# A 352-byte pad behind h's tile in place of 376 bytes, in a two-layer retention and convolution trunk on one core

## The chip, the core and the metric

The kernel runs on one core of a Trainium2 chip. The time is the device time of one execution in microseconds (us); the figure that counts is the median over runs. Before the change it is 2637.42 us (three runs, 2634.95 to 2639.48).

## What is computed

A trunk of two layers works on 256 tokens of width 2048 in f32. Layer 0 mixes tokens by multi-scale retention, layer 1 by a short gated convolution; each is followed by a SwiGLU feed-forward part (FFN), and every part is framed by an RMS norm with shift, scale and gate, which come from the conditioning vector `c`:

```python
for i in range(DEPTH):
    mod = (c_act @ w_mod[i] + b_mod[i])[:, None, :]
    sh1, sc1, g1, sh2, sc2, g2 = jnp.split(mod, 6, axis=-1)
    h = (rms_norm(x, norm1_g[i]) * (1.0 + sc1) + sh1)
    y = retention_mixer(...) if i == 0 else short_conv_mixer(...)
    x = x + g1 * y
    h = (rms_norm(x, norm2_g[i]) * (1.0 + sc2) + sh2)
    x = x + g2 * swiglu(h, ffn_w_in[i], ffn_w_out[i])
return rms_norm(x, final_g)
```

Nearly all of the work is products of an activation with a weight matrix: `h @ w_in` (retention: 2048 to 12288 columns, convolution: 2048 to 6144, FFN: 2048 to 11264) and then `mid @ w_out` back to 2048 columns.

## The kernel before

**Numbers in two parts.** Each f32 value is held as a high part that TensorE takes in its f32r type and the rest as a low part. A product is then three products: high by high, high by low, low by high. An activation tile is 128 rows by 2 x 256: the high part of the 256 tokens and behind it the low part, 2048 bytes in each partition. Weights arrive from memory as `raw` tiles of 128 x 2048, and `prepare` (lines 298 to 317) makes of each half of one a tile `hi` (ScalarE, line 313) and a tile `lo` (VectorE, line 316) of 128 x 1024, in four buffers each. A tile holds eight blocks of 128 x 128, each 512 bytes long in a partition, and `take` hands them out in the order of use.

**The products.** The loop of `product` (lines 348 to 366) makes one pair of matmuls for each weight block: line 358 loads the block of `hi` as the stationary operand and streams all 512 columns of the activation tile past it, line 361 loads the block of `lo` and streams the 256 columns of the high part. `packed` (lines 376 to 404) makes three matmuls of 256 columns instead (lines 398 to 400), for most of the retention's projections and for the last column of an output product; where the weights are 512 wide it hands over to `by_token` (lines 373 to 375), which loads `h` and streams the weights. `normed` (lines 506 to 553) has a form of its own for the first six columns after a norm, lines 529 to 531.

**The activations.** `h` is the normed input of each part. It is read by the input products of convolution and FFN, as the tile named `h` in lines 358 and 361. Their results become the `mid` tiles, 22 at a time in the FFN and 16 in the convolution, and the output products read those (`output`, lines 555 to 578). In the retention the tiles between input and output product are called `rm` (`rm_tile`, line 634); the output product over 32 of them comes in two parts, each after four heads.

**Where the tiles lie.** Pools are laid out in SBUF one behind the other, in the order in which they are opened, and each tile in them starts at a multiple of 32 bytes. The order is: constants, work tiles, the weights' pool (`raw`, `hi`, `lo`), the pool of `h` and, behind that, whatever is in use at the time: the retention's tiles (`rm`, `sin`, `cos`, the start's own `raw`, `q`, `k`, `v`, `sp`, `decay`, `sg`, `o`) or later those of FFN and convolution (`mid`, `silu`, `m`, `cu`, `y`, `out`). The pool of `h` holds three tiles: `aside` of 8 words (line 486), `h` itself, 17 x 514 words or 34952 bytes (line 487), and `beside`, which nobody reads or writes (line 488). The offsets in a partition are:

| tile | first byte | distance from the first `hi` | remainder by 512 |
|---|---|---|---|
| first `hi` (all `hi` and `lo` lie at multiples of 4096 from it) | 84832 | 0 | 0 |
| `h`, as FFN and convolution read it (`rows_at(0)`) | 117632 | 32800 | 32 |
| `h`, as the retention reads it (`rows_at(EARLIER)`, 480 bytes on) | 118112 | 33280 | 0 |
| first tile behind the pad; `rm` and `mid` tiles follow every 2048 bytes | 152992 | 68160 | 64 |

From here on "a distance of 64" means this remainder. The weights step by 512 bytes from block to block and the activations by 2048 from tile to tile, so the remainder stays what it is through a whole product.

**The order of work.** TensorE's instructions run in the order in which they are written out. The other engines' instructions are put in order by a planner; at the start, VectorE's and ScalarE's order is written out too. `prepare` runs two tiles ahead of TensorE (`AHEAD`). All loads go through SyncE's queue: `raw` of the weights, and `raw` of `w_mod` for the 192 columns of the modulation, each of which is one long VectorE instruction (line 247, and line 657 at the start, where the `raw` tile lies behind the pad).

Of the kernel before, what the change touches and what calls it, by code (L numbers as in the profile page):

```python
# [10 lines left out]
F32 = mybir.dt.float32  # L11
# [6 lines left out]
P = 128  # L18
# [170 lines left out]
def trunk(ctx: ExitStack, tc: tile.TileContext, x_in, c_in, pos_in, w_mod, cols_in, tab_in, w_all, out):  # L189
# [290 lines left out]
    hpool = ctx.enter_context(tc.tile_pool(name="hpool", bufs=1))  # L480
# [4 lines left out]

    hpool.tile([P, LEFT], F32, tag="aside", name="aside")
    h_all = hpool.tile([P, (KT + 1) * (ENDS + 2 * S)], F32R, tag="h", name="h")
    hpool.tile([P, 94], F32, tag="beside", name="beside")

    def rows_at(o):  # L490
        return [
# [575 lines left out]
```

## Time and profile before

| | |
|---|---|
| median of three runs | 2637.42 us |
| profiled execution | 2638.99 us, of which the span from first to last instruction is 2637.2 |
| granted TensorE clock | 0.997 over the span |
| TensorE busy | 2603.5 us |
| VectorE, ScalarE, GpSimd busy | 1989.3, 1248.5 and 149.3 us |
| moved by DMA | 687.58 MB |

A row of the page's groups gives line, engine and operation, the tiles (written from read), the shapes, the count, the busy time of the group in us, the mean duration of one instruction in ns, and the idle time of the engine ahead of the group with what ended it. The busy time counts a moment once, however many instructions of the group run in it. "PE" is TensorE's matmuls, "PEld" its weight loads, "DVE" VectorE, "ACT" ScalarE, "SP" SyncE. A view by windows gives, for stretches of the span, the busy time of each engine with its count of instructions, the granted clock, the busy share of the DMA engines and what they moved.

### The profile page before, as it was taken

How to read it: one execution, taken by the hardware profiler on the slowest of the kernel's cores; microseconds unless marked ns; L12 is line 12 of the kernel's file. 1: busy time of each engine (PE TensorE's matmuls, PEld its weight loads, DVE VectorE, ACT ScalarE, POOL GpSimd, SP SyncE). 2: the span in 40 equal slices, each digit the busy share in tenths (PEclk: the TensorE clock that was granted, in tenths of full speed). 3: DMA queues.
4: the chain of work that ended last, by engine and by line, in shares of the span. 5: the costliest groups of instructions: out<-in, count | busy, mean ns of one | idle time of the engine just before them, and what ended most of it. 6: DMA issues, size and time to landing. Idle time of an engine off the chain costs nothing.

```text
span 2637.2 us, 38238 instructions
## 1 busy us (share of the span) xinstructions
PE 2603.5 (99%) x15220; PEld 2304.2 (87%) x15220; DVE 1989.3 (75%) x2527; ACT 1248.5 (47%) x1788; POOL 149.3 (6%) x230
## 2 busy tenths in 40 slices
PE   7999999999999999999999999999999999999998
PEld 5988889888889888888888898888998888888887
DVE  7888878777698877777777889888886665555554
ACT  5544443444456444344444454444554443444443
POOL 0000001110000011110100001100000000000000
PEclk9999999999999999999999999999999999999999
DMA  9976768777686877777777768777777755555553
GB/s 399 384 278 244 254 249 299 276 267 276 238 307 249 315 284 280 261 285 287 287 273 276 265 226 323 284 285 257 254 273 269 255 217 184 191 192 191 189 181 126
DMA packets 96950, 687.58 MB, mean 261 GB/s; under 512 B 10753, under 2 KB 12545, under 8 KB 13825
## 3 DMA queue, kind: packets, MB, share of 16 engines
q1 hardware_dynamic: 96770, 685.13, 70.2%
q8 instruction: 119, 1.95, 0.3%
q14 instruction: 61, 0.50, 0.1%
HBM read 682.99 MB, written 2.10 MB: 260 GB/s over the span
## 4 chain that ended last, share of the span: by engine, by line
PE 75%; issue 20%; DVE 3%; DMA 2%; ACT 1%; POOL 0%; DVEq 0%; ACTq 0%; POOLq 0%
PE bank L358 34%; PE bank L361 18%; PE bank L373 4%; PE bank L374 4%; PE bank L375 4%; PE bank L400 2%; PE bank L399 2%; PE bank L398 2%; PE bank L529 1%; PE bank L531 1%; PE bank L530 1%; DVE raw L657 1%; DMA raw<-w_all 1%; DVE lo L316 1%; DMA raw<-w_mod 1%
## 5 line engine op out<-in xcount | busy, mean ns | idle before, releaser
L316 DVE TENSOR_TENSOR lo<-raw,hi 128x1024 fp32r<-128x1024 f32 x912 | 1112.0, 1222 | 544.9 <-ACT hi L313 543.7
L313 ACT CAST hi<-raw 128x1024 fp32r<-128x1024 f32 x912 | 953.6, 1050 | 1078.9 <-PE bank L358 648.3
L358 PE MATMUL bank<-h,hi 128*128 128x512 f32 x3296 | 1142.9, 390 | 0.0
L361 PE MATMUL bank<-h,lo 128*128 128x256 f32 x3296 | 929.5, 282 | 0.0
L358 PEld LDWEIGHTS bank<-h,hi 128*128 128x128 f32 x3296 | 618.8, 188 | 129.6
L361 PEld LDWEIGHTS bank<-h,lo 128*128 128x128 f32 x3296 | 622.9, 189 | 0.0
L358 PE MATMUL bank<-mid,hi 128*128 128x512 f32 x1604 | 566.2, 395 | 0.0
L361 PE MATMUL bank<-mid,lo 128*128 128x256 f32 x1604 | 452.1, 282 | 1.1 <-DVE lo L316 1.1
L247 DVE SCALAR_TENSOR_TENSOR raw<-raw,cb 128x2048 f32<-128x2048 f32 x160 | 365.3, 2283 | 14.9 <-DMA raw<-w_mod 14.6
L358 PEld LDWEIGHTS bank<-mid,hi 128*128 128x128 f32 x1604 | 301.4, 188 | 72.5
L361 PEld LDWEIGHTS bank<-mid,lo 128*128 128x128 f32 x1604 | 301.2, 188 | 1.5 <-DVE lo L316 1.5
L373 PE MATMUL bank<-hi,h 128*128 128x512 f32 x512 | 202.0, 395 | 0.0
L374 PE MATMUL bank<-lo,h 128*128 128x512 f32 x512 | 201.1, 393 | 0.0
L375 PE MATMUL bank<-hi,h 128*128 128x512 f32 x512 | 200.5, 392 | 0.0
L358 PE MATMUL bank<-rm,hi 128*128 128x512 f32 x496 | 175.3, 396 | 0.0
L400 PE MATMUL bank<-h,lo 128*128 128x256 f32 x512 | 146.3, 286 | 9.3 <-DVE lo L316 9.3
L398 PE MATMUL bank<-h,hi 128*128 128x256 f32 x512 | 145.9, 285 | 2.5 <-ACT h L685 2.5
L399 PE MATMUL bank<-h,hi 128*128 128x256 f32 x512 | 145.9, 285 | 0.5 <-DVE h L686 0.5
L361 PE MATMUL bank<-rm,lo 128*128 128x256 f32 x496 | 139.7, 282 | 0.0
L375 PEld LDWEIGHTS bank<-hi,h 128*128 128x128 f32 x512 | 96.8, 189 | 21.0
L358 PEld LDWEIGHTS bank<-rm,hi 128*128 128x128 f32 x496 | 93.2, 188 | 22.4
L373 PEld LDWEIGHTS bank<-hi,h 128*128 128x128 f32 x512 | 97.0, 189 | 18.0
(154 smaller groups left out, 2248.7 us busy)
## 6 DMA issues: line engine op xcount, KB each, us to landing
raw<-w_all SPq DMA_DIRECT2D x456, 1024.0 KB, 4.8
raw<-w_mod SPq DMA_DIRECT2D x192, 1024.0 KB, 5.0
x<-x_in SPq DMA_DIRECT2D x4, 512.0 KB, 5.6
out<-out SPq DMA_DIRECT2D x5, 256.0 KB, 3.4
decay<-tab_in SPq DMA_DIRECT2D x8, 128.0 KB, 2.2
out<-out SPq DMA_DIRECT2D x3, 128.0 KB, 2.5
out<-out SPq DMA_DIRECT2D x1, 384.0 KB, 2.7
cols<-cols_in SPq DMA_DIRECT2D x1, 160.0 KB, 8.7
```

Of the source, the lines that this page charges most:

```text
L247: nc.vector.scalar_tensor_tensor(raw, raw, 1.0, cb, op0=ALU.mult, op1=ALU.mult, accum_out=total)
L313: nc.scalar.copy(hi, raw)
L316: nc.vector.tensor_tensor(lo, raw, hi.bitcast(F32), op=ALU.subtract)
L358: nc.tensor.matmul(pt, hi, h, start=fresh and k == g.ks[0], stop=False, skip_group_check=True)
L361: nc.tensor.matmul(pt[:, 1, :], lo, h[:, 0, :], start=False, stop=last and k == g.ks[-1], skip_group_check=True)
L373: nc.tensor.matmul(o, ht[:, 0, :], hi, start=first, stop=False)
L374: nc.tensor.matmul(o, ht[:, 0, :], lo, start=False, stop=False)
L375: nc.tensor.matmul(o, ht[:, 1, :], hi, start=False, stop=last)
L398: nc.tensor.matmul(pt, hi, h[:, 0, :], start=first, stop=False, skip_group_check=True)
L399: nc.tensor.matmul(pt, hi, h[:, 1, :], start=False, stop=False, skip_group_check=True)
L400: nc.tensor.matmul(pt, lo, h[:, 0, :], start=False, stop=last, skip_group_check=True)
L529: nc.tensor.matmul(pt, hi, high, start=k == 0, stop=False, skip_group_check=True)
```

## The change

The pad `beside` has 88 words instead of 94, 352 bytes instead of 376. With starts at multiples of 32 bytes, 352 bytes take 352 and 376 take 384, so that every tile behind the pad starts 32 bytes lower and has a remainder of 32 instead of 64 (or 96, instead of 128, behind `cu`). No instruction, no operand's shape and no order is written differently.

```diff
     hpool.tile([P, LEFT], F32, tag="aside", name="aside")
     h_all = hpool.tile([P, (KT + 1) * (ENDS + 2 * S)], F32R, tag="h", name="h")
-    hpool.tile([P, 94], F32, tag="beside", name="beside")
+    hpool.tile([P, 88], F32, tag="beside", name="beside")
```

## The prediction

> **What bounds the kernel now.** I read the page's busy times and slices first, to see whether one engine sets the time.
>
> ```profile
> span 2637.2 us, 38238 instructions
> PE 2603.5 (99%) x15220; PEld 2304.2 (87%) x15220; DVE 1989.3 (75%) x2527; ACT 1248.5 (47%) x1788; POOL 149.3 (6%) x230
> PEclk9999999999999999999999999999999999999999
> ```
>
> TensorE is busy 99% of the span at the full clock, so it does, and the question is what sets the distance in time from one matmul to the next. The change moves no instruction; it moves operands. Next come the groups of matmuls, page and groups by line:
>
> ```profile
> L358 PE MATMUL bank<-h,hi 128*128 128x512 f32 x3296 | 1142.9, 390 | 0.0
> L361 PE MATMUL bank<-h,lo 128*128 128x256 f32 x3296 | 929.5, 282 | 0.0
> L358 PE MATMUL bank<-mid,hi 128*128 128x512 f32 x1604 | 566.2, 395 | 0.0
> L361 PE MATMUL bank<-mid,lo 128*128 128x256 f32 x1604 | 452.1, 282 | 1.1 <-DVE lo L316 1.1
> L358 PE MATMUL bank<-rm,hi 128*128 128x512 f32 x496 | 175.3, 396 | 0.0
> ```
>
> The same two lines of code, with the same shapes and counts of columns, run on three kinds of activation tile. A matmul of line 358 lasts longer (390 to 396 ns) than the time to the next one of its line, so within a product they overlap without a gap, and the busy time of the line divided by its count is the time that one pair takes, both lines together. That is 1142.9 / 3296 = 0.3468 us a pair on `h`, 566.2 / 1604 = 0.3530 on `mid`, 175.3 / 496 = 0.3534 on `rm`. `h` lies at a distance of 32 from the weights, `mid` and `rm` at 64.
>
> The timeline, TensorE's rows alone, shows the same pairs one by one: a product on `mid`, one on `h`, and a second product on `mid`.
>
> ```profile
> 1059.04 0.40 PE L358 MATMUL bank<-mid,hi 128*128 128x512 f32 x1
> ...
> 1059.40 0.40 PE L358 MATMUL bank<-mid,hi 128*128 128x512 f32 x1
> ...
> 1059.76 0.39 PE L358 MATMUL bank<-mid,hi 128*128 128x512 f32 x1
> ...
> 1060.10 0.40 PE L358 MATMUL bank<-mid,hi 128*128 128x512 f32 x1
> ...
> 1061.16 0.40 PE L358 MATMUL bank<-mid,hi 128*128 128x512 f32 x1
> ```
>
> ```profile
> 900.12 0.39 PE L358 MATMUL bank<-h,hi 128*128 128x512 f32 x1
> ...
> 900.47 0.39 PE L358 MATMUL bank<-h,hi 128*128 128x512 f32 x1
> ...
> 900.82 0.39 PE L358 MATMUL bank<-h,hi 128*128 128x512 f32 x1
> ...
> 901.16 0.39 PE L358 MATMUL bank<-h,hi 128*128 128x512 f32 x1
> ```
>
> ```profile
> 1839.76 0.39 PE L358 MATMUL bank<-mid,hi 128*128 128x512 f32 x1
> ...
> 1841.86 0.39 PE L358 MATMUL bank<-mid,hi 128*128 128x512 f32 x1
> ```
>
> On `mid` the pairs go 0.36, 0.36, 0.34 and over again: six take 2.12 us, 0.3533 each, with no wait marked. On `h` they go 0.35, 0.35, 0.34, three in 1.04, 0.3467 each. In the third stretch, in the convolution's output product, six take 2.10, 0.350 each. So at a distance of 64 there are two paces, and which of them a product falls into isn't set by the distance alone.
>
> Last, the windows of whole products: is anything but TensorE late in them? The columns are the window, its length, the busy times of PE, PEld, DVE, ACT and POOL with their counts, the granted clock, the DMA share and GB/s.
>
> ```profile
> 711.40:779.00 67.60, 67.60 (x386) 58.85 (x384) 63.17 (x96) 35.05 (x56) 2.06 (x6) 1.00 0.73 267
> 820.90:1031.50 210.60, 210.60 (x1216) 186.68 (x1216) 167.37 (x204) 106.73 (x168) 18.34 (x28) 1.00 0.79 294
> 1031.70:1156.00 124.30, 124.30 (x705) 108.20 (x705) 90.78 (x99) 46.81 (x47) 12.87 (x20) 1.00 0.74 272
> 1793.20:1878.30 85.10, 83.96 (x479) 73.14 (x479) 74.88 (x107) 42.28 (x60) 2.37 (x7) 1.00 0.75 271
> 2130.90:2255.10 124.20, 124.20 (x705) 108.31 (x704) 67.97 (x77) 46.65 (x46) 0.00 (x0) 1.00 0.52 187
> 2255.30:2499.10 243.80, 243.80 (x1408) 216.15 (x1407) 139.07 (x175) 117.04 (x174) 0.00 (x0) 1.00 0.53 189
> ```
>
> Row three is the first half of the first FFN's output, 352 pairs on `mid`, row five the same in the second layer. In row three VectorE is busy for 73% and DMA at 0.74, in row five for 55% and at 0.52, and TensorE takes 124.3 and 124.2 us. What the other engines and the loads do doesn't touch the pace. Row two is 608 pairs on `h`, 210.6 / 608 = 0.3464, row six 704 pairs, 0.3463.
>
> **The change, part by part.** It removes and adds no operation and no wait. It moves every operand behind the pad by 32 bytes. The operands fall into four classes.
>
> First, the 1604 pairs on `mid` and 496 on `rm`. Their distance becomes 32, that of `h`. At `h`'s pace they gain 1604 x (0.3530 - 0.3468) = 9.9 us and 496 x (0.3534 - 0.3468) = 3.3 us, 13.2 together. Could they land elsewhere? The trace has 3296 pairs at 32, in five stretches (both halves of each FFN's input product and the convolution's), and both quoted windows give the same pace to 0.1 ns; the slower pace that a run of pairs at 64 can also fall into, 0.350, is my bound on the other side: 2100 x (0.3531 - 0.350), the mean of the two tiles, is 6.5 us. I take 13.2.
>
> The Trainium skill has a rule that speaks against this step: "SBUF — State Buffer", section "Who interferes with whom", gives TensorE one read port for the moving operand and another, independent one for weight loads, lets only the port pair of VectorE and GpSimd contend, and says that TensorE never waits on anyone. By it the distance between weights and activations can't matter and the sum is 0. The trace doesn't bear that out: 0.3468 and 0.3530 are the same instructions, of an engine that waits for nothing. What in the chip makes the difference no row tells.
>
> Second, matmuls of 256 columns (lines 398 to 400) on `mid` and `rm`, 76 sets of three. No row has this form at 32:
>
> ```profile
> L399 PE MATMUL bank<-h,hi 128*128 128x256 f32 x512 | 145.9, 285 | 0.5 <-DVE h L686 0.5
> L399 PE MATMUL bank<-mid,hi 128*128 128x256 f32 x60 | 16.8, 280 | 0.0
> ```
>
> At a distance of 0 one lasts 285 ns, at 64 280. If the step to 32 lengthened each by those 5 ns, 228 would cost 1.1 us; if it shortened them as much, they would give 1.1. I take 0: line 361, of 256 columns too, lasts 282 ns at 32 and at 64.
>
> Third, matmuls whose operands both lie behind the pad: the scores (`q`, `k`), the retention's outputs (`v`, `sp`). Both move, the distance stays, cost 0. The 64 transposes of `o` against the identity do change their distance; at those 5 ns each, 0.3 us either way, taken at 0.
>
> Fourth, operands of VectorE, ScalarE and DMA. The one VectorE instruction that the trace has on both sides of the pad is the long one of the modulation:
>
> ```profile
> L247 DVE SCALAR_TENSOR_TENSOR raw<-raw,cb 128x2048 f32<-128x2048 f32 x160 | 365.3, 2283 | 14.9 <-DMA raw<-w_mod 14.6
> ...
> L657 DVE SCALAR_TENSOR_TENSOR raw<-raw,cb 128x2048 f32<-128x2048 f32 x32 | 72.9, 2284 | 0.3 <-DMA raw<-w_mod 0.2
> ```
>
> With `raw` at a distance of 0 it takes 2283 ns, at 64 behind the pad 2284. I take 0 for all of these; one ns on each of VectorE's 2527 instructions would be 2.5 us of an engine that is a quarter idle.
>
> What is late next? A product that runs 2% faster asks for `hi` and `lo` 2% sooner. Preparation is ahead of TensorE and waits for its buffers, as the view of waits shows (us in total, times, longest):
>
> ```profile
> ACT hi L313 <- PE bank L358: 648.3, 428, 2.0
> ```
>
> ScalarE waits 648.3 us in all for matmuls of line 358 to set a buffer free, while matmuls of the pairs wait 1.1 us for `lo`. Where VectorE is nearly full the gain could be given back: the retention's second output (63.17 of 67.60 us) and the convolution's (74.88 of 85.10), 248 and 240 pairs, 248 x 0.0066 + 240 x 0.0062 = 3.1 us if all of it went. I expect most of it to stay, since those windows' products on `rm` wait for nothing and the other's wait is the 1.1 us. The clock is no cover that can go: at `h`'s pace it is granted in full already.
>
> The sum: 2638.99 - 13.2 = 2625.8 us for the profiled execution, span 2624.0. That execution is 1.6 us above the median, so the median becomes 2637.42 - 13.2 = 2624.2.
>
> **Rivals.** *The second pace.* `mid` and `rm` at 32 settle at about 0.350, gain 6.5 us, 2630.9. For it: at 64 one product did fall into another pace. Against: no window on `h` shows a second one. *Nothing happens.* The pace belongs to the product, not to the distance: output products gather in banks that are opened earlier and read two by two, or the moved tiles still differ from `h` in what matters, or the pad's size doesn't round as laid out in the table. Time 2637.4; the skill's rule of independent ports gives the same. For it: `h` and `mid` also differ in which stage they serve, and no tile is seen at both distances. Against: the code is the same and the rows show no wait. *Slower.* The distance counts by more than the remainder of 512: `h` lies 64 x 512 + 32 from the weights, `mid` afterwards 133 x 512 + 32, an odd multiple, and that could be the worse case. If every pair then took the longest step seen, 0.36, the price is 2100 x (0.36 - 0.3531) = 14.5 us and the time 2652; it turns from gain to loss where a pair takes over 0.353. Against: blocks step by 512 and tiles by 2048, so the pairs on `h` go through all such multiples, and their steps are even.
>
> **How the numbers follow.** The forecast has 0.80, the second pace 0.07, no effect 0.09, slower 0.04. A measurement of this kernel tells about 0.2%, 5.3 us, from no change: forecast and second pace lie beyond it, so faster 0.87, same 0.09, slower 0.04. Low end: 2624.2 less the 1.4 of the second class and the transposes, less the 2.5 by which the lowest run lies under the median, about 2620. High end: the second pace, 2631, which also holds the 3.1 of gains given back and the 1.4.
>
> **What would show it.** In the profile after, line 358 on `mid` would have a mean of 390 ns instead of 395 and a busy time of 1604 x 0.3468 = 556 us, on `rm` 390 and 172; on `h` both stay at 390 and 1142.9. The two windows of 352 pairs on `mid` would shrink from 124.3 to 122.1 us, the steps of the timeline become 0.35, 0.35, 0.34. TensorE's waits for `lo` should grow by under 3 us. I am wrong if line 358 on `mid` keeps 395 ns or its steps 0.36 (no effect), if its mean is near 393 (second pace), or if pairs reach 0.346 while the span shrinks by much less than 13 us: then the waits say where it went.

## The result and the profile after

The changed kernel takes 2625.12 us, the median of six runs (2621.43 to 2626.3), against 2637.28 us in six runs of the kernel before (2634.95 to 2639.8): 12.2 us less. The ratio is 0.995, with a 95% interval of 0.9938 to 0.9963, so the gain, half a per cent, is clear of the noise. The span of the profiled execution falls from 2637.2 to 2623.5 us, by more, since the execution profiled before lay 1.7 us above its median and the one after 0.2. Each engine's instructions stand in the same order as before.

The page after, span and busy times:

```profile
span 2623.5 us, 38238 instructions
...
PE 2589.9 (99%) x15220; PEld 2303.6 (88%) x15220; DVE 1988.6 (76%) x2527; ACT 1247.9 (48%) x1788; POOL 150.1 (6%) x230
```

TensorE has lost 13.6 us of busy time and the span 13.7. DVE and ACT have lost 0.7 and 0.6 us; what has become shorter is TensorE's own work. The groups of matmuls show where:

```profile
L358 PE MATMUL bank<-h,hi 128*128 128x512 f32 x3296 | 1142.8, 390 | 0.0
...
L358 PE MATMUL bank<-mid,hi 128*128 128x512 f32 x1604 | 556.3, 390 | 0.0
L361 PE MATMUL bank<-mid,lo 128*128 128x256 f32 x1604 | 452.4, 282 | 0.8 <-DVE lo L316 0.8
...
L373 PE MATMUL bank<-hi,h 128*128 128x512 f32 x512 | 201.9, 394 | 0.0
...
L358 PE MATMUL bank<-rm,hi 128*128 128x512 f32 x496 | 172.5, 390 | 0.0
```

Busy time by count, as before, gives 556.3 / 1604 = 0.3468 us a pair on `mid` and 172.5 / 496 = 0.3478 on `rm`, where it was 0.3530 and 0.3534; `h` has kept its 0.3467. The mean of line 358 is 390 ns on all three. The gains are 9.9 us on `mid` and 2.8 on `rm`, 12.7 of the 13.6. Another 0.7 comes from lines 373 to 375, which had 202.0, 201.1 and 200.5 us and have 201.9, 200.9 and 200.1, although their operands are where they were.

TensorE's rows of the timeline on `mid` and the windows of the two halves of 352 pairs:

```profile
1058.77 0.39 PE L358 MATMUL bank<-mid,hi 128*128 128x512 f32 x1
...
1059.12 0.39 PE L358 MATMUL bank<-mid,hi 128*128 128x512 f32 x1
...
1059.46 0.39 PE L358 MATMUL bank<-mid,hi 128*128 128x512 f32 x1
...
1059.81 0.39 PE L358 MATMUL bank<-mid,hi 128*128 128x512 f32 x1
```

```profile
1028.50:1150.50 122.00, 122.00 (x705) 108.17 (x704) 90.95 (x100) 46.79 (x47) 13.69 (x20) 1.00 0.74 276
...
2121.80:2243.80 122.00, 122.00 (x705) 108.16 (x704) 67.93 (x77) 46.77 (x47) 0.00 (x0) 1.00 0.52 190
```

The steps of 0.36, 0.36, 0.34 have become 0.35, 0.34, 0.35: three pairs take 1.04 us, as on `h`. Both windows have shrunk to 122.0 us, again to the same length beside a VectorE that is busy for 75% of the one and 56% of the other.

Preparation is still ahead; in the view of waits ScalarE's wait for a free buffer has shrunk by 15.9 us, a little more than the gain, and TensorE's largest wait for `lo` has hardly moved (9.3 us before):

```profile
ACT hi L313 <- PE bank L358: 632.4, 422, 2.0
...
PE bank L400 <- DVE lo L316: 9.5, 6, 2.2
```

### The profile page after: what moved, and what is told of

Same layout as the page of the kernel before. It is cut to its first block, busy times and chain, and to the rows that moved or that the text cites. A ratio compares the mean times of both kernels' runs of the same rounds, so it can differ in the third digit from the quotient of the medians.

```text
span 2623.5 us, 38238 instructions
## 1 busy us (share of the span) xinstructions
PE 2589.9 (99%) x15220; PEld 2303.6 (88%) x15220; DVE 1988.6 (76%) x2527; ACT 1247.9 (48%) x1788; POOL 150.1 (6%) x230
## 4 chain that ended last, share of the span: by engine, by line
PE 75%; issue 20%; DVE 2%; DMA 2%; ACT 1%; POOL 0%; DVEq 0%; ACTq 0%; POOLq 0%
PE bank L358 34%; PE bank L361 18%; PE bank L373 4%; PE bank L374 4%; PE bank L375 4%; PE bank L400 2%; PE bank L399 2%; PE bank L398 2%; PE bank L529 1%; PE bank L531 1%; PE bank L530 1%; DVE raw L657 1%; DVE lo L316 1%; DMA raw<-w_all 1%; DMA raw<-w_mod 1%
## 5 line engine op out<-in xcount | busy, mean ns | idle before, releaser
L358 PE MATMUL bank<-h,hi 128*128 128x512 f32 x3296 | 1142.8, 390 | 0.0
L358 PE MATMUL bank<-mid,hi 128*128 128x512 f32 x1604 | 556.3, 390 | 0.0
L373 PE MATMUL bank<-hi,h 128*128 128x512 f32 x512 | 201.9, 394 | 0.0
L374 PE MATMUL bank<-lo,h 128*128 128x512 f32 x512 | 200.9, 392 | 0.0
L375 PE MATMUL bank<-hi,h 128*128 128x512 f32 x512 | 200.1, 391 | 0.0
L358 PE MATMUL bank<-rm,hi 128*128 128x512 f32 x496 | 172.5, 390 | 0.0
L374 PEld LDWEIGHTS bank<-lo,h 128*128 128x128 f32 x512 | 97.1, 190 | 17.5
```

Of the source, the lines that this page charges most:

```text
L358: nc.tensor.matmul(pt, hi, h, start=fresh and k == g.ks[0], stop=False, skip_group_check=True)
L373: nc.tensor.matmul(o, ht[:, 0, :], hi, start=first, stop=False)
L374: nc.tensor.matmul(o, ht[:, 0, :], lo, start=False, stop=False)
L375: nc.tensor.matmul(o, ht[:, 1, :], hi, start=False, stop=last)
```

## The experiments

The theory was that the distance in bytes between the weight blocks and the activation that is streamed, by its remainder, sets the pace of the pairs. The rivals: the absolute address does (before the change `mid` lay 32 bytes off a multiple of 64, after it at one, where `h` lay all along), or a product's place in the kernel, or a larger modulus than 512. In all times that follow, the kernel before was run on the same chip.

**A sweep of distances, alone.** A program without the trunk streams 32 activation tiles past the same weight buffers, each 32 bytes further from them than the last (like the two sweeps below it was executed once, at a granted clock of 1.00):

```python
for i in range(N):
    acts.append(pool.tile([P, 1024], F32R, tag=f"off{32 * i}b", name=f"off{32 * i}b"))
    if i < N - 1:
        pool.tile([P, 8], F32, tag=f"gap{i}", name=f"gap{i}")
```

> This program leaves the trunk out: after one load it makes only matmuls, on constant weights in four hi and four lo buffers laid out as in the kernel, against 32 activation tiles whose distance from the weights rises by 32 bytes, from 0 to 992 (the tile's name tells it). Four forms follow one another, each over all distances: pairs as in lines 358 and 361 in rising order (96 a tile), the same pairs in falling order, sets of three as in lines 398 to 400 (64 a tile), and sets as in lines 373 to 375 (32 a tile). Nothing else runs and nothing waits. Theory, the distance by its remainder of 512 sets the pace: pairs take 0.3467 us at 32 and between 0.350 and 0.3533 at 64, sets of three 3 x 0.1200 at 0 and 3 x 0.1167 at 32, and the tiles from 512 on repeat those from 0 on. Rival, the absolute address: two paces that take turns from tile to tile, since each lies 32 bytes further by a multiple of 64. Rival, the product's place in the kernel: all tiles the same. Rival, more than the remainder of 512 counts: the tiles from 512 on differ from those from 0 on.

The view by tile gives, for each group, the least, median and greatest duration in ns and the start of the first and the last. Lines 55 and 56 are the pairs in rising order, line 60 the same in falling order; 96 starts have 95 steps between them.

```profile
L55 PE MATMUL bank<-off32b,hi x96: 390/390/397, 51.8 to 84.7; 128*128 128x512 f32 x96
L55 PE MATMUL bank<-off64b,hi x96: 388/397/398, 85.1 to 118.6; 128*128 128x512 f32 x96
L55 PE MATMUL bank<-off96b,hi x96: 392/394/398, 119.0 to 152.2; 128*128 128x512 f32 x96
...
L55 PE MATMUL bank<-off160b,hi x96: 391/392/397, 186.3 to 219.2; 128*128 128x512 f32 x96
L55 PE MATMUL bank<-off192b,hi x96: 392/397/398, 219.6 to 253.1; 128*128 128x512 f32 x96
...
L55 PE MATMUL bank<-off256b,hi x96: 393/398/403, 287.4 to 321.0; 128*128 128x512 f32 x96
L55 PE MATMUL bank<-off288b,hi x96: 390/390/399, 321.3 to 354.3; 128*128 128x512 f32 x96
```

```profile
L55 PE MATMUL bank<-off544b,hi x96: 390/390/399, 590.8 to 623.8; 128*128 128x512 f32 x96
```

```profile
L60 PE MATMUL bank<-off256b,hi x96: 391/391/396, 1869.4 to 1902.3; 128*128 128x512 f32 x96
```

At 32 the 95 steps take 32.9 us, 0.346 each, at 64 33.5, 0.353: with next to nothing else running, the two paces of the kernel. 96 lies between, 160 is as good as 32, 192 as slow as 64. The tiles at 32, 96 and 160 all start at multiples of 64, and their paces differ, which speaks against that alignment as the cause; and not every tile is the same, so a product's place in a kernel isn't the whole cause either. 288 and 544, at 33.0 us, are as 32: the pattern repeats after 256 bytes already, and an odd multiple of 512 is no worse. One row was expected by nobody: at 256 the pairs take 0.354 in the rising order and 0.346 in the falling one. The multiples of 256 agree in this: 256, 512 and 768 take 33.6 us each in the rising order, where a tile at 224 by the remainder ran ahead, and 768, 512, 256 and 0 take 32.9 each in the falling one, where a tile at 32 did.

**The same distances at other addresses.**

```diff
     wpool = ctx.enter_context(tc.tile_pool(name="wpool", bufs=PART_BUFS))
+    wpool.tile([P, 8], F32, tag="ahead", name="ahead", bufs=1)
```

> The changed kernel with a tile of 32 bytes ahead of the weights, so that weights, h and all behind lie 32 bytes higher and no distance changes. The mid tiles then lie at the very addresses that they had before the change (152992 and on), at a distance of 32 in place of 64. Theory, distance: pairs on mid, rm and h stay at 0.3467 us, mean of line 358 on mid 390 ns, time as after the change, 2625. Rival, absolute address: line 358 on mid and rm is back at 395 and 396 ns, 2638; and h, which now lies where alignment by 64 is lost too, would add up to 3296 x 6.2 ns, some 20 us, 2658.

The groups; line 359 is line 358 of the other kernels:

```profile
L359 PE MATMUL bank<-h,hi 128*128 128x512 f32 x3296 | 1142.9, 390 | 0.0
...
L359 PE MATMUL bank<-mid,hi 128*128 128x512 f32 x1604 | 556.3, 390 | 0.0
...
L359 PE MATMUL bank<-rm,hi 128*128 128x512 f32 x496 | 172.5, 390 | 0.0
```

With `mid` at the very bytes where it lay before the change, its pairs keep the fast pace to the tenth of a microsecond. The absolute address is out. The time is 2628.28 us (2623.26 to 2629.86), a ratio of 0.9957 (0.9941 to 0.9974). Its median is 3 us above that of the changed kernel; the runs of the two overlap, and the groups of pairs have no part in it. By its rows lines 374 to 376, which are 373 to 375 of the other, take 202.5, 201.5 and 200.6 us, 1.7 more in all; why isn't shown.

**h at 64.**

```diff
-LEFT, ENDS, EARLIER = 8, 2, 120
+LEFT, ENDS, EARLIER = 16, 2, 112
...
-    hpool.tile([P, 88], F32, tag="beside", name="beside")
+    hpool.tile([P, 80], F32, tag="beside", name="beside")
```

> The changed kernel with 16 words ahead of h in place of 8 and a pad of 320 bytes: h as FFN and convolution read it lies at a distance of 64, as the retention reads it at 0 as before, rm and mid at 32. Theory, distance: line 358 on h goes from 390 to about 395 ns and its pairs from 0.3467 to 0.3530 us (0.350 at least), 3296 x 6.2 ns = 20 us more (11 at least), so 2636 to 2646; mid and rm stay at 390 ns. Rival, the pace belongs to the product and its place in the kernel: h keeps 390 ns and the time 2625.

```profile
L358 PE MATMUL bank<-h,hi 128*128 128x512 f32 x3296 | 1164.7, 396 | 0.0
...
L358 PE MATMUL bank<-mid,hi 128*128 128x512 f32 x1604 | 556.3, 390 | 0.0
```

The input products now take the slow pace, 1164.7 / 3296 = 0.3534, which they had never shown, and the output products keep the fast one. The time is 2646.5 us, at the upper end of what was expected, 21.4 above the changed kernel, and slower than the kernel before: ratio 1.0034 (1.0023 to 1.0045). The pace goes with the distance, not with the product.

**Half of the change undone.**

```diff
     mpool = ctx.enter_context(tc.tile_pool(name="mpool", bufs=1))
+    mpool.tile([P, 8], F32, tag="before", name="before")
```

> The changed kernel with a tile of 32 bytes ahead of the FFN's and the convolution's tiles alone: mid lies at a distance of 64 again, at the addresses that it had before the change; rm stays at 32. Theory: line 358 on mid 395 ns and busy for 566 us, on rm 390 ns and 172.5 us, the time 9.9 us over that after the change, 2635: the two parts add up. Rival, the gain hangs on rm or on other tiles behind the pad: time near 2625 with mid's pairs slow, or mid's pairs fast.

```profile
L358 PE MATMUL bank<-mid,hi 128*128 128x512 f32 x1604 | 566.9, 396 | 0.0
...
L358 PE MATMUL bank<-rm,hi 128*128 128x512 f32 x496 | 172.7, 391 | 0.0
```

2635.22 us, 10.1 above the changed kernel, against 9.9 worked out. The ratio to the kernel before, 0.9991 (0.9982 to 1.0001), leaves 2.4 us for `rm`; the interval holds 1, so the time alone doesn't show it. By the rows `rm` has 175.3 - 172.7 = 2.6, and `mid` takes 0.7 more than the 566.2 before. These 0.7 us lie in the convolution's output product. Before the change TensorE waited in the middle of it for `lo` for 1.1 us, and the 159 pairs behind that wait took (1878.1 - 1823.0) / 158 = 0.349 us each where the 81 ahead of it took 0.353. Here the wait at the same place is 0.25 us long, and the 159 pairs behind it keep 0.353, on the same bytes.

**A larger pad.** `beside` with 120 words puts `rm` and `mid` at 160.

```diff
-    hpool.tile([P, 88], F32, tag="beside", name="beside")
+    hpool.tile([P, 120], F32, tag="beside", name="beside")
```

> The pad behind h has 120 words, 480 bytes, more than either kernel: mid and rm lie at a distance of 160, 128 bytes above where the change puts them. By the sweep pairs at 160 take 0.3467 us, as at 32, and sets of three 0.3520. Theory: line 358 on mid and rm 391 to 392 ns, busy 556 and 172 us, time as after the change, 2625. Rival, a lower place or less memory helps, or 32 alone is good: mid's pairs at 0.350 or more and 2630 to 2640.

```profile
L358 PE MATMUL bank<-mid,hi 128*128 128x512 f32 x1604 | 556.4, 392 | 0.0
```

2625.84 us, ratio 0.9953 (0.9938 to 0.9968): as the changed kernel, with more memory used and the tiles higher up than in either. The sweep's map holds in the kernel, and 32 is not the only good value.

**The retention's h at 32 too.** If 32 is good for pairs, is it for the other forms?

```diff
-LEFT, ENDS, EARLIER = 8, 2, 120
+LEFT, ENDS, EARLIER = 8, 2, 128
```

> The changed kernel with h, as the retention reads it, 32 bytes further (EARLIER 128), at a distance of 32 in place of 0; the rest stays. By the sweep, a set of three of lines 398 to 400 goes from 0.3600 to 0.3533 us at 32 and a set of lines 373 to 375 from 0.6800 to 0.7001. Theory, the sweep's map holds in the kernel: 512 sets of each, 512 x (0.0201 - 0.0067) = 6.9 us more where TensorE is the bound, so 2626 to 2632, and the mean of lines 373 to 375 rises while that of lines 398 to 400 falls. Rival, 32 is the better distance for every form: lines 373 to 375 keep 392 to 394 ns and the time falls by up to 512 x 0.0067 = 3.4 us, to 2622.

```profile
L373 PE MATMUL bank<-hi,h 128*128 128x512 f32 x512 | 204.0, 398 | 0.0
...
L398 PE MATMUL bank<-h,hi 128*128 128x256 f32 x512 | 144.4, 282 | 2.5 <-ACT h L685 2.5
```

Line 398 gets faster, 285 to 282 ns, line 373 slower, 394 to 398, and the time is 2628.69 us, 3.6 more than after the change. So the good distance belongs to the form of the product: where `h` is the stationary operand and the weights are streamed, 0 is better than 32.

**Finer, and hi against lo.** A second sweep moves the `lo` blocks against the `hi` blocks as well.

> Leaves the trunk out, as the first sweep did: only pairs as in lines 358 and 361, 64 for each case. Eight shifts of the lo tiles against the hi tiles (0 to 224 bytes by 32, by the remainder of 256), each with 16 distances of the activations from hi (0 to 240 by 16), and at shift 0 the 16 distances between them (8 to 248). The names of the tiles tell shift and distance. Theory, each matmul has its own price by the distance between what it streams and the block that is loaded meanwhile: the pace depends on distance and shift together, with the same values at 32-byte steps and shift 0 as in the first sweep (0.3467 at 32 and 160, 0.3533 at 64 and 192), and some pair of them may fall under 0.3467. Rival, 0.3467 is the least that a pair takes, whatever the distance: no case under it.

```profile
L54 PE MATMUL bank<-off64b,hi0b x64: 391/397/400, 116.1 to 138.4; 128*128 128x512 f32 x64
...
L54 PE MATMUL bank<-off64b,hi64b x64: 388/389/394, 833.0 to 854.4; 128*128 128x512 f32 x64
```

The second number in a tile's name is the shift of `lo`. With the activation at 64 in both rows, 63 steps take 22.3 us without a shift and 21.4 with `lo` 64 bytes on: 0.354 and 0.340. So 0.3467 is not the least, and shift and distance count together. In the kernel this is a gap between the buffers and other pads:

```diff
-LEFT, ENDS, EARLIER = 8, 2, 120
+LEFT, ENDS, EARLIER = 8, 2, 112
...
+        if not n:
+            wpool.tile([P, 16], F32, tag="gap", name="gap", bufs=1)
         lo = wpool.tile([P, HALF], F32R, tag="lo", name=name("lo"))
...
-    hpool.tile([P, LEFT], F32, tag="aside", name="aside")
...
-    hpool.tile([P, 88], F32, tag="beside", name="beside")
+    hpool.tile([P, 24], F32, tag="beside", name="beside")
```

> The changed kernel with 64 bytes between the hi tiles and the lo tiles, no tile ahead of h and a pad of 96 bytes: counted from hi by the remainder of 256, lo lies at 64, h as FFN and convolution read it at 64, rm and mid at 64, h as the retention reads it at 0. In the fine sweep this is one of two cases under 0.3467: 0.3400 us a pair. Theory, the shift of lo against hi and the distance together set the pace: line 358's pairs at 0.3400 on h, mid and rm, 5396 x 6.67 ns = 36 us less than the changed kernel, 2589, or more where the forms of the retention (lines 373 to 375 and 398 to 400), for which no shift was tried, lose: 512 sets of each, at 10 ns a set 5 us. Rival, 0.3400 was a pace that a product only falls into from that sweep's order: pairs at 0.3467 to 0.3533 and 2625 to 2660. Rival, VectorE becomes the bound: pairs at 0.3400 between growing waits for lo, time falls by less.

Groups, and then two windows of the same kernel, from 1620 to 1780 us (the convolution's input product) and from 1220 to 1380 (an FFN's); line 360 is line 358 of the others:

```profile
L360 PE MATMUL bank<-h,hi 128*128 128x512 f32 x3296 | 1127.1, 390 | 0.0
...
L360 PE MATMUL bank<-mid,hi 128*128 128x512 f32 x1604 | 546.5, 389 | 0.0
```

```profile
L360 PE MATMUL bank<-h,hi 128*128 128x512 f32 x446 | 156.1, 395 | 0.0
```

```profile
L360 PE MATMUL bank<-h,hi 128*128 128x512 f32 x471 | 160.2, 389 | 0.0
```

2599.63 us (2598.11 to 2602.52), ratio 0.9849 (0.9833 to 0.9866). The median is 25.5 us below the changed kernel, the span of the profiled execution 22.8 (2623.5 - 2600.7). The pairs on `h`, `mid` and `rm` have lost more, 1142.8 + 556.3 + 172.5 - 1127.1 - 546.5 - 169.5 = 28.5; in the retention lines 375 to 377, 373 to 375 of the changed kernel, have become slower, from 394, 392 and 391 ns to 398, 396 and 395. The expected 36 was too much, because in the first window the convolution's input product ran at 156.1 / 446 = 0.350 while the FFN's ran at 160.2 / 471 = 0.340, with the same operands' distances. It had not begun so. TensorE's timeline, 43 us behind that product's first pair:

```profile
1585.10 0.39 PE L360 MATMUL bank<-h,hi 128*128 128x512 f32 x1
...
1585.44 0.39 PE L360 MATMUL bank<-h,hi 128*128 128x512 f32 x1
...
1585.97 0.39 PE L360 MATMUL bank<-h,hi 128*128 128x512 f32 x1
...
1586.32 0.40 PE L360 MATMUL bank<-h,hi 128*128 128x512 f32 x1
```

Up to here 129 pairs have followed one another every 0.340 us. One comes 0.53 us after the last, 0.19 late, with no wait marked, and the 543 from there to the product's end follow every 0.350, (1775.7 - 1586.0) / 542. The convolution's output product goes on at that pace for 81 pairs and is back at 0.340 behind a wait of 1.1 us for `lo`. These 624 pairs, at 0.010 us each, are 6.2 us of the 7.5 that are missing. So a delay inside a product can change its pace. To see whether what ran ahead decides it too, the third sweep enters the same pair from ever other stretches.

> Leaves the trunk out: stretches of 64 pairs or sets. First sets of three as in lines 398 to 400, then sets as in lines 373 to 375, both with lo shifted by 64 and distances 0 to 240 by 16; then, so that a stretch is entered from ever other stretches, by turns a pair at every distance with lo shifted by 64, the pair at 64 with lo shifted by 64, a set of three at every distance without shift, and the pair at 192 with lo shifted by 192. Theory: the pairs at 64 and 192 with lo shifted as much take 0.3400 us whatever ran ahead of them. Rival, two paces as at distance 0 in the first sweep: some of their stretches at 0.3467 or 0.3533, their mean above 0.3400. For the other forms no value is expected; the least is sought.

Two windows, one around each of two stretches of 64 pairs at 64 with `lo` shifted by 64; the first follows a stretch at distance 0, the second one at 32:

```profile
L54 PE MATMUL bank<-off64b,hi64b 128*128 128x512 f32 x64 | 21.8, 389 | 0.0
```

```profile
L54 PE MATMUL bank<-off64b,hi64b 128*128 128x512 f32 x64 | 22.4, 395 | 0.0
```

The same pair, on the same bytes, takes 21.8 / 64 = 0.341 or 22.4 / 64 = 0.350 us, and stays at it for the whole stretch: the theory's "whatever ran ahead" fell. Of the 16 stretches of this pair, each behind a stretch at another distance, 12 take the faster pace and 4 the slower. Each entry was made once, so this sweep alone doesn't tell the stretch ahead from chance; the multiples of 256 in the first sweep, where the same entry gave the same pace three times of three and four of four, speak for the stretch ahead.

This sweep also gave the other forms' values with that shift, from which two more kernels were made; they differ in where the retention reads `h` (EARLIER 76 and 108).

> The version with lo 64 bytes on and h, rm and mid at 64, and h as the retention reads it at a distance of 112 in place of 0 (EARLIER 76). In the sweep of the other forms with that shift a set of three takes 0.3467 us at 112 in place of 0.3598 at 0, and a set of lines 373 to 375 0.6933 in place of 0.6957. Theory, the map holds in the kernel: up to 512 x (0.0131 + 0.0024) = 7.9 us less than at 0, 2592, less what the retention waits for VectorE. Rival, the retention is bound by VectorE or falls into other paces: 2597 to 2600.

> The same version with h, as the retention reads it, at a distance of 240 (EARLIER 108): 0.3533 a set of three and 0.6866 a set of lines 373 to 375, up to 512 x (0.0065 + 0.0091) = 8.0 us less than at 0, 2592. Rival as for the distance of 112: 2597 to 2600.

They take 2595.94 us (2595.46 to 2597.48; ratio 0.9842, 0.9829 to 0.9856) and 2590.69 (2589.65 to 2595.54; ratio 0.9828, 0.9815 to 0.9841), where 2592 was expected of both. The second is the fastest of all, 34.4 us below the changed kernel. Its groups:

```profile
L360 PE MATMUL bank<-h,hi 128*128 128x512 f32 x3296 | 1121.0, 389 | 0.0
...
L375 PE MATMUL bank<-hi,h 128*128 128x512 f32 x512 | 200.8, 392 | 0.7 <-ACT hi L315 0.7
```

Its `h` pairs are at 1121.0 / 3296 = 0.3401, the convolution's among them, although their distances are those of the kernel that had most of them at 0.350 and only what the retention reads was moved: in this execution the 672 pairs follow one another without a late one. Why none came late isn't shown. The kernel with 112 has the same 1121.0 there, but its line 375 takes 203.4 us, as much as at 0 (203.5), so the sweep's value for that form, 0.6933 a set against 0.6957, did not carry over. Its pairs on `mid` and `rm` take 547.2 and 171.5 us, where the fastest kernel has 545.7 and 169.7: 208 pairs on `rm`, and on `mid` the 159 behind a wait of 0.9 us in the convolution's output product, run at 0.350.

## Why the prediction was right

**The terms.** The forecast was 13.2 us less and 2624.2 us; the median is 2625.12, 12.2 less, and the span fell by 13.7. The term for `mid`, 9.9, is met to the tenth. The term for `rm`, 3.3, came out at 2.8. It took the pace of `h` for the one after, and dividing a busy time by a count overstates the pace where a group is broken into short pieces, since each piece ends with a whole matmul: the 496 pairs on `rm` come in 8 pieces, each of which adds some 390 - 347 = 43 ns, 0.3 us of the 0.5 that are missing, and after the change the division still gives 0.3478 on `rm` against 0.3468 on `mid`. What was missing there came from lines 373 to 375, 0.7 us, which stood in no term. Their operands had not moved, and why they got shorter isn't shown; to that extent the closeness of the span is luck.

**The cause.** That distance, not stage, sets the pace was read from one line of code at two distances. The experiments with `h` at 64 and with all tiles 32 bytes up show it: the pace moved with the distance and ignored product and address. The Trainium skill's rule in "SBUF — State Buffer" (section "Who interferes with whom"), by which nothing should have happened, is not borne out: 0.346 and 0.353 us stand side by side in a program that runs hardly anything beside matmuls.

**The rivals.** The second pace was real, and its condition was only half understood. I had it as something that a product at 64 can fall into, and read it as 0.350 from six pairs. It is 0.349 over the 159 pairs of that stretch, so that the rival would have been worth 2100 x (0.3531 - 0.349) = 8.6 us and not 6.5. The stretch began behind a wait inside the product, and the run with `mid` back at 64 shows that with a shorter wait there it doesn't begin. The third sweep shows two paces for the shifted pair, and the first that a distance of 256 has two as well; at 64 without a shift the first sweep had 0.353 in either order and never 0.349. At 32, without a shift, no run showed a second one, which is why the size came out. The slower rival, an odd multiple of 512, is ruled out by the tile at 544.

**What was taken at 0.** Sets of three on `mid` and `rm` went from 280 to 279 ns, inside their bounds. VectorE's moved operands cost nothing: its busy time fell by 0.7 us. Nothing of the gain was given back in the two stretches where VectorE is nearly full; the convolution's output pairs waited 0.8 us for `lo` instead of 1.1.

What stays open is the place in the chip where a streamed operand and a weight load meet. That they meet is argued from the fact that shift and distance count together; no run shows it directly. Nor does any row tell why a delay can change the pace of all pairs behind it.

## What to carry to other kernels

When TensorE is busy throughout, divide the busy time of a line by its count for each tile that it reads: two paces for one shape, with no wait beside them, can mean that addresses cost time, and a pad of some bytes is then worth trying. Sweep the distance between stationary and streamed operand, for each form of product by itself and over one period of 256 bytes, and take a good value only after it has held in the kernel, since a product can have two paces and one late pair can change them.

## What the runs showed of the hardware

- In the sweeps, pairs of a 512-column and a 256-column f32r matmul took 0.340 to 0.354 us where nothing was varied but the order and the remainder by 256 of the distances between `hi`, `lo` and the streamed tile.
- At the same distances a product can run at 0.340 or 0.350 us a pair. The two paces came behind different stretches, and a delay inside a product changed the pace: behind one pair that was 0.19 us late, 543 pairs went at 0.350 where 129 had gone at 0.340.
- The best distance for `h` as the stationary operand (0 rather than 32) is not the best for `h` as the streamed one.
